# A first weights' page loaded in two halves, the rows' squares behind their splits, and a priority for the values' products of a gated attention

## The chip, the cores and the metric

The kernel runs on one core of one Trainium2 chip. The metric is device time in microseconds (us). Engines are named as the profile names them: PE is TensorE (PEld its weight load), DVE is VectorE, ACT is ScalarE, POOL is GpSimd, SP is SyncE, which here only issues DMAs.

## The reference, cut to what matters

Two transformer blocks follow each other on one sequence of 512 rows and 1024 columns, all in float32. Block 1 puts 16 meta tokens in front and mixes a state-space model with a differential attention; block 2 is a gated linear attention with a mixture of experts, then a sparse attention with another. The change touches the beginning of block 1 and the beginning of block 2:

```python
# block 1
hn = rmsnorm(h, norm1_g)                    # h * rsqrt(mean(h*h) + eps) * g
u, q, k, v, g_ssm, g_att = split(hn @ w_in) # 528 rows, K = 1024
y_ssm = s5_mixer(u, ...)                    # x = B u; complex scan over the rows; y = C s + d u; gelu; GLU
o = diff_attention(q, k, v, lam, slopes)
h = h + (sigmoid(g_ssm) * (y_ssm @ w_ssm_out) + sigmoid(g_att) * (y_att @ w_att_out)) @ w_o
h = h + conv_glu_ffn(rmsnorm(h), ...)
...
# block 2, gated linear attention (gla_mixer)
q, k, v, g_low, r = split(x @ w_in)
log_a = log_sigmoid(g_low @ w_gate_up + b_gate) / 16
b = cumsum(log_a within a chunk of 64 rows)
q_dec = q * exp(b);  k * exp(-b);  k * exp(b_last - b)
o = where(causal, q_dec @ (k * exp(-b)).T, 0) @ v + q_dec @ states
```

## The kernel before, in words

Rows are kept transposed: a tile is 128 of the 1024 features by all rows (528 in block 1, `T`; 512 in block 2, `S`). Every float32 product is made of three products of rounded numbers: each operand is split into a high part (ACT rounds it) and a low part (DVE subtracts), and `mm3` (L394, L395, L396) issues high x high, low x high and high x low, all added up in PSUM.

**Weights** arrive as a stream of pages of 128x2048 (1 MB; tag `wr`, three buffers, `Stream.ahead`, DMA at L334). `Tiles.next` takes 1024 columns at a time and splits them at L369: a CAST on ACT, then a TENSOR_TENSOR on DVE, called the lo split below. There are two such split pairs in flight, and the split is put 1000 places ahead of the program's order. The order of instructions on each engine is fixed when the kernel is built: a scheduler takes the program in the order written, where `tc.high_priority(offset=n)` moves what stands in it n places forward, and models when buffers come free. On the chip an engine keeps to that order and waits where something is not ready.

**Block 1's start.** SP issues the eight loads of `hT` (L454, tiles `hx`), three pages of weights, and the small tables. For each of the eight k, ACT makes the high part `xh` (L461), DVE the low part `xl` (L462), ACT the square (L464), and PE adds up the squares of all k against a tile of ones (L466, `ss`). `rstd_wide` turns that sum into 1/rms (L473 on ACT, L474 RECIPROCAL on DVE). The rows aren't scaled before the product with the weights: the result is multiplied by 1/rms when it is taken out of PSUM (L360). The first four output tiles (`mm`, 48 matmuls of 264 columns each) are `u`; the query and gate tiles follow as filler between the steps of the state-space model.

**The state-space model** works in four groups (`ssm_main`, m = 0 to 3) and three steps each: transposes; then `xps` (L673), a copy by ACT (L675), eight products and two scans by DVE (L680 and around it), six more products, and four DMAs that turn the state round (L688); then `yps` (L700, L701), a copy by ACT (L702), `yt` (L708) and gelu (L709). Fillers stand between the steps. After the last filler come the key and value products (`kv`, 512 columns), whose PSUM tiles are `kv_2269`, `kv_2270` and so on in the orders below.

**Block 2's start.** The rows are split again; eight small products give `glo`, and four more (`z`, L1100) the gate's argument. DVE adds the bias (L1101), ACT makes Abs, Exp and Ln over 128x2048 (L1102, L1103, L1104), DVE four products and four scans (L1108, L1109), ACT three exponentials (L1111, L1112, L1118). The values' products, `stream_tm`, take two halves of 512 columns: each is 96 matmuls of 512 columns into four PSUM banks (`tm`), which are then copied to `vtok` at L1145, two banks by ACT and two by DVE. The second half needs the banks of the first from its 14th matmul on. After them come the eight tiles of queries and keys (`mm`); the first query tile is taken out of PSUM by DVE at L1150.

Of the kernel before, what the change touches and what calls it, by code (L numbers as in the profile page):

```python
# [14 lines left out]
AF = mybir.ActivationFunctionType  # L15
ALU = mybir.AluOpType
# [5 lines left out]
KD = 8  # L22
# [246 lines left out]
def build(ctx, tc, I, out, dbg=None):  # L269
    nc = tc.nc  # L270
    V, A, G, TE = nc.vector, nc.scalar, nc.gpsimd, nc.tensor
# [13 lines left out]
    def sb(n, tag, dt=F32, bufs=1):  # L285
        return ar.get(n, tag, dt, bufs)

    def p2(name):
        return pp_.tile([P, 2, 512], F32, tag="p2", name=name, bufs=3)
# [10 lines left out]
    def load_c(name, dt=F32, eng=None):  # L300
        ap = I[name]
        t = gc.tile([ap.shape[0], ap.shape[1]], dt, tag=name, name=name)
        (eng or nc.sync).dma_start(out=t, in_=ap)
        return t

    def load_a(name, dt=F32):

        ap = I[name]
        t = sb(ap.shape[1], name, dt)[:ap.shape[0]]
        nc.sync.dma_start(out=t, in_=ap)  # L310
        return t
# [6 lines left out]
    class Stream:  # L318
# [9 lines left out]
        def ahead(self, n):  # L328

            for i in range(self.used, min(self.used + n, len(self.src))):  # L330
                if i not in self.tiles:
                    ap, bufs = self.src[i]
                    t = sb(2048, "wr", F32, bufs)
                    ld = nc.sync.dma_start(out=t[:, :ap.shape[1]], in_=ap)  # L334
                    self.later(ld)
                    if i in self.hold:
                        tc.add_manual_dep(ld.ins, self.hold[i], mybir.DependencyInfo(mybir.DependencyClass.Sync, mybir.DependencyReason.DATA),
                                          reason="the rows that are needed sooner go first")
                    self.tiles[i] = t

        def later(self, ld):

            if self.behind is not None:
                after(ld, self.behind)
# [6 lines left out]
    st = Stream()  # L351
# [7 lines left out]
    def tt(o, a, b, op, eng=None):  # L359
        return (eng or V).tensor_tensor(o, a, b, op=op)  # L360
# [32 lines left out]
    def mm3(o, a, b, start, stop):  # L393
        TE.matmul(o, a[0], b[0], start=start, stop=False)  # L394
        TE.matmul(o, a[0], b[1], start=False, stop=False)  # L395
        TE.matmul(o, a[1], b[0], start=False, stop=stop)  # L396
# [24 lines left out]
    def pairs(h, l):  # L421
        def x(k, sl):
            return h[k][:, sl], l[k][:, sl]
        return x
# [26 lines left out]
    hx = [sb(T, "hx", bufs=8) for _ in range(KD)]  # L451
    with tc.manual_schedule(engines={mybir.EngineType.SP}):
        for k in range(KD):
            nc.sync.dma_start(out=hx[k], in_=I['hT'][:, k])  # L454
        st.ahead(WR)
        s_a, s_d = load_c('s_a'), load_c('s_d')
        s_b, s_c = load_a('s_b'), load_a('s_c')
        blk, b16 = load_c('c_blk'), load_c('c_b16')
        g2, glu_b, qks, cw, cb = (load_c(n) for n in ('g2', 'glu_b', 'qks', 'cw', 'cb'))
    for k in range(KD):  # L460
        A.activation(xh[k], hx[k], AF.Identity, scale=g1[:, k:k + 1])  # L461
        V.scalar_tensor_tensor(xl[k], hx[k], g1[:, k:k + 1], xh[k].bitcast(F32), op0=ALU.mult, op1=ALU.subtract)  # L462
        t = sb(T, "t1", bufs=3)
        A.activation(t, hx[k], AF.Square)  # L464
        for j, sl in enumerate(HC):
            TE.matmul(pss[:, j, :264], ones, t[:, sl], start=k == 0, stop=k == KD - 1)  # L466
    drop("hx")
# [109 lines left out]
    for g_ in range(2):  # L577
        for ri in range(2):
            nc.scalar.dma_start(out=bst[64 * ri:64 * ri + 64, g_ * 256:(g_ + 1) * 256],
                                in_=bb[64 * g_:64 * g_ + 64, ri * 256:(ri + 1) * 256])  # L580
# [190 lines left out]
    def proj_kv():  # L771
        acc = [p1("kv0"), p2("kv1"), p2("kv2")]
        o = [acc[0], acc[1][:, 0], acc[1][:, 1], acc[2][:, 0], acc[2][:, 1]]
        for k in range(KD):
            w = wt.next(512)
            for c, (k0, n) in enumerate(kch):
                mm3(o[c], x1(k, slice(k0, k0 + P)), w, k == 0, k == KD - 1)
        return o

    o = proj_kv()  # L780
# [24 lines left out]
    o = proj_kv()  # L805
# [128 lines left out]
    for j in range(16):  # L934
        i, h = j // 4, j % 4
# [62 lines left out]
    for m in range(8):  # L998
        o = sb(T, "h1", bufs=3)[:, :MID]
# [9 lines left out]
        else:  # L1009
            t = sb(T, "t1", bufs=3)[:, :MID]  # L1010
# [9 lines left out]
    hx = pairs(hh, hl)  # L1020
# [3 lines left out]
    for m in range(NFF):  # L1024
# [4 lines left out]
        c = sb(S, "t1", bufs=3)  # L1029
# [11 lines left out]
    for m in range(8):  # L1041
        t = sb(S, "t1", bufs=3)
# [45 lines left out]
    for k in range(KD):  # L1088
        split(x2[k], x2h[k], x2l[k])
        c = k % 4  # L1090
# [31 lines left out]
    def stream_tm(x, mid=None):  # L1122

        acc = [p2("tm0"), p2("tm1")]
        o = [acc[0][:, 0], acc[0][:, 1], acc[1][:, 0], acc[1][:, 1]]
        for k in range(KD):
            w = wt.next(512)
            for t in range(4):
                mm3(o[t], x(k, slice(t * P, (t + 1) * P)), w, k == 0, k == KD - 1)
            if mid and k == 3:  # L1130
                mid()
        return o
# [6 lines left out]
    drop_tiles("xf")  # L1139
    drop("rst", "cu", "gt1", "glo", "w_gl", "w_gu")  # L1140
    vtok = [sb(1024, f"vtok{t}") for t in range(4)]
    for nh in range(2):
        o = stream_tm(xx)
        for t in range(4):
            (A.copy if t % 2 else V.tensor_copy)(vtok[t][:, nh * 512:(nh + 1) * 512], o[t])  # L1145
    for m in range(8):
        ps = dense_fm(KD, xx, [slice(0, S)], p1u)[:, 0]
        sl = slice((m % 4) * S, (m % 4 + 1) * S)
# [561 lines left out]
    o = stream_tm(x4a)  # L1710
# [11 lines left out]
    o = stream_tm(x4a)  # L1722
# [210 lines left out]
    for nh in range(2):  # L1933
        o = stream_tm(x4a, first_half if nh else None)
# [66 lines left out]
```

## Time and profile before

| | |
|---|---|
| median of 3 runs | 1920.88 us (1920.16 to 1924.55) |
| profiled execution, its own time | 1918.51 us |
| its span | 1916.7 us |
| mean granted clock of TensorE, share of full speed | 0.949 |
| PE busy | 1743.3 us, 91% of the span |
| DVE, ACT, POOL busy | 64%, 46%, 9% |

The span is what the profile sees between the first and the last instruction; the time of the same execution is 1.8 us longer. PE is busy for nine tenths of the span, so a step is worth what it takes from PE's idle time or from the stretches in which its clock is at half.

### The profile page before, as it was taken

What the parts mean: (1) busy time and instruction counts of PE and PEld (TensorE: products, weight loads), DVE (VectorE), ACT (ScalarE), POOL (GpSimd) and SP (SyncE); (2) the same over time, 40 slices, a digit from 0 to 9 for tenths busy, and PEclk for the clock granted to TensorE, in tenths of its full rate; (3) what the DMA queues carried; (4) which work ended last, traced back from release to release, by engine and by line L of the source; (5) the groups of instructions that cost most, each with busy time, mean ns of one, the idle gap of its engine ahead of it and who ended that gap; (6) DMA issues with size and microseconds to landing.
All of it is one profiled execution on the core that took longest, in us unless ns stands there. A gap on an engine that the chain in (4) does not pass through costs nothing.

```text
span 1916.7 us, 27254 instructions
## 1 busy us (share of the span) xinstructions
PE 1743.3 (91%) x10719; PEld 1480.1 (77%) x10719; DVE 1221.8 (64%) x2276; ACT 874.1 (46%) x1397; POOL 173.3 (9%) x140
## 2 busy tenths in 40 slices
PE   8999999899999999999999799949998999859990
PEld 7899877798989988877888578738886777647870
DVE  7855368776555643253347889874337777669985
ACT  4233346433333332243223288843236665628881
POOL 2310000022000000000000122110000000012213
PEclk9999999899999999999999799979898999879995
DMA  5335221242322233212225599752230003539953
GB/s 194 110 110 140 89 88 65 63 160 90 108 89 89 88 135 114 95 66 88 88 88 206 188 325 380 281 217 77 85 136 23 1 12 123 208 126 338 380 224 140
DMA packets 69205, 269.73 MB, mean 141 GB/s; under 512 B 22144, under 2 KB 24720, under 8 KB 44240
## 3 DMA queue, kind: packets, MB, share of 16 engines
q1 hardware_dynamic: 52384, 246.38, 35.9%
q0 software_dynamic: 9216, 16.80, 2.4%
q10 hardware_dynamic: 7472, 4.76, 1.2%
q8 instruction: 85, 1.39, 0.3%
q14 instruction: 48, 0.39, 0.1%
HBM read 249.62 MB, written 30.43 MB: 146 GB/s over the span
## 4 chain that ended last, share of the span: by engine, by line
PE 63%; DVE 6%; ACT 3%; DMA 2%; issue 2%; POOL 0%; SPq 0%; POOLq 0%; DVEq 0%; ACTq 0%
PE mm L396 8%; PE mm L395 8%; PE mm L394 8%; PE psh L395 3%; PE psh L396 3%; PE psh L394 3%; PE tm L394 2%; PE tm L395 2%; PE tm L396 2%; PE npo L1920 2%; PE npt L1908 2%; PE op L395 2%; PE op L394 2%; PE op L396 2%; PE xgt L1431 1%
## 5 line engine op out<-in xcount | busy, mean ns | idle before, releaser
L369 ACT CAST pg<-pg 128x1024 fp32r<-128x1024 f32 (+2 forms) x437 | 427.4, 1007 | 554.1 <-PE mm L395 224.9
L369 DVE TENSOR_TENSOR pg<-pg,pg 128x1024 fp32r<-128x1024 f32 (+2 forms) x437 | 503.0, 1176 | 264.6 <-ACT pg L369 251.4
L396 PE MATMUL mm<-pg,pg 128*128 128x258 f32 (+2 forms) x1504 | 483.0, 322 | 4.0 <-DVE pg L369 4.0
L394 PE MATMUL mm<-pg,pg 128*128 128x258 f32 (+2 forms) x1504 | 484.9, 323 | 1.4 <-ACT pg L888 0.7
L395 PE MATMUL mm<-pg,pg 128*128 128x258 f32 (+2 forms) x1504 | 482.9, 321 | 0.0
L394 PEld LDWEIGHTS mm<-pg,pg 128*128 128x128 f32 x1504 | 287.6, 191 | 28.0 <-ACT pg L886 2.8
L396 PEld LDWEIGHTS mm<-pg,pg 128*128 128x128 f32 x1504 | 286.8, 191 | 24.9 <-DVE pg L369 4.7
L395 PEld LDWEIGHTS mm<-pg,pg 128*128 128x128 f32 x1504 | 287.4, 191 | 21.2 <-issue 0.4
L360 DVE TENSOR_TENSOR pg<-mm,pg 128x256 f32<-128x256 f32 (+3 forms) x138 | 66.2, 510 | 138.8 <-PE mm L396 138.8
L395 PE MATMUL psh<-pg,pg 128*128 128x512 f32 x256 | 106.4, 416 | 2.3 <-DVE pg L369 2.3
L394 PE MATMUL psh<-pg,pg 128*128 128x512 f32 x256 | 101.9, 398 | 0.0
L396 PE MATMUL psh<-pg,pg 128*128 128x512 f32 x256 | 101.3, 396 | 0.0
L394 PE MATMUL tm<-pg,pg 128*128 128x512 f32 x192 | 76.4, 408 | 4.6 <-ACT pg L1145 4.6
L395 PE MATMUL tm<-pg,pg 128*128 128x512 f32 x192 | 77.3, 403 | 1.2 <-DVE pg L369 1.2
L396 PE MATMUL tm<-pg,pg 128*128 128x512 f32 x192 | 76.1, 396 | 0.0
L360 DVE TENSOR_TENSOR pg<-pg,pg 128x512 f32<-128x512 f32 (+12 forms) x103 | 57.1, 575 | 24.9 <-ACT pg L675 10.6
L1892 ACT ACTIVATE pg<-ns,nmx 128x512 f32<-128x512 f32 (+3 forms) x128 | 66.3, 531 | 11.4 <-DVE nmx L1888 7.2
L1888 DVE TENSOR_REDUCE nmx<-ns 128x2 f32<-128x1024 f32 (+3 forms) x48 | 50.1, 1043 | 17.3 <-PE ns L1885 17.1
L360 DVE TENSOR_TENSOR pg<-pg 128x64 f32<-128x64 f32 (+8 forms) x127 | 49.5, 411 | 17.4 <-ACT pg L1033 15.4
L395 PEld LDWEIGHTS psh<-pg,pg 128*128 128x128 f32 x256 | 48.9, 191 | 13.2 <-DVE pg L369 4.4
L1425 POOL DMA_INDIRECT pg<-xd,idx x32 | 38.1, 1189 | 219.2 <-DVE wts L360 122.7
L394 PEld LDWEIGHTS psh<-pg,pg 128*128 128x128 f32 x256 | 48.8, 191 | 11.4
(440 smaller groups left out, 2960.9 us busy)
## 6 DMA issues: line engine op xcount, KB each, us to landing
pg<-in_w_moe_dram SPq DMA_DIRECT2D x96, 1024.0 KB, 10.4
pg<-in_w_up_dram SPq DMA_DIRECT2D x22, 1024.0 KB, 4.8
pg<-in_w_dn_dram SPq DMA_DIRECT2D x11, 1024.0 KB, 4.9
pg<-in_w_g_dram SPq DMA_DIRECT2D x8, 1024.0 KB, 5.5
pg<-in_w_go_dram SPq DMA_DIRECT2D x8, 1024.0 KB, 4.8
pg<-yd SPq DMA_DIRECT2D x16, 512.0 KB, 7.8
pg<-in_w_n_dram SPq DMA_DIRECT2D x8, 1024.0 KB, 6.8
pg<-in_w_no_dram SPq DMA_DIRECT2D x8, 1024.0 KB, 4.8
```

What stands on the lines that cost most here:

```text
L360: return (eng or V).tensor_tensor(o, a, b, op=op)
L369: return A.copy(h, src), V.tensor_tensor(l, src, h.bitcast(F32), op=ALU.subtract)
L394: TE.matmul(o, a[0], b[0], start=start, stop=False)
L395: TE.matmul(o, a[0], b[1], start=False, stop=False)
L396: TE.matmul(o, a[1], b[0], start=False, stop=stop)
L1425: ld = G.indirect_dma_start(out=xg, out_offset=None, in_=self.xd, in_offset=bass.IndirectOffsetOnAxis(ap=self.idx[:, e:e + 1], axis=0), bo ...
L1431: TE.transpose(ps[:, k // 4, (k % 4) * P:(k % 4 + 1) * P], xg[:, k * P:(k + 1) * P], ident)
L1888: V.tensor_reduce(mx, sc, axis=AX.X, op=ALU.max, negate=True)
L1892: A.activation(pp[:, r, br], sc[:, r, br], AF.Exp, bias=mx[:, r, br:br + 1], accum_out=se[:, r, br:br + 1])
L1908: TE.transpose(src[:, r, br, c * P:(c + 1) * P], pp[:, r, br, c * P:(c + 1) * P], ident)
L1920: TE.matmul(o_[64 * r:64 * r + 64], vsw[:, c * 512 + br * 256 + g * 64:c * 512 + br * 256 + (g + 1) * 64], pts[r][:, br, c * P:(c + 1) * P ...
```

## The change

Three edits. The first page of `w_u` is loaded in two halves: the first 1024 columns right behind the first two loads of `hT`, the other 1024 behind the eighth. The loop over the eight tiles writes all splits first and all squares in a second loop, and the squares of even k go to DVE as a product. The two halves of the values' products and the copies of their results get a priority of 1000 places.

```diff
+                    c = ap.shape[1] // 2 if i == 0 else ap.shape[1]
+                    ld = nc.sync.dma_start(out=t[:, :c], in_=ap[:, :c])
                     self.later(ld)
+                    if i == 0:
+                        self.first = t, ap, c
...
+        def rest(self):
+            t, ap, c = self.first
+            nc.sync.dma_start(out=t[:, c:2 * c], in_=ap[:, c:])
...
         for k in range(KD):
             nc.sync.dma_start(out=hx[k], in_=I['hT'][:, k])
+            if k == 1:
+                st.ahead(1)
+        st.rest()
         st.ahead(WR)
...
     for k in range(KD):
         A.activation(xh[k], hx[k], AF.Identity, scale=g1[:, k:k + 1])
         V.scalar_tensor_tensor(xl[k], hx[k], g1[:, k:k + 1], xh[k].bitcast(F32), op0=ALU.mult, op1=ALU.subtract)
+    for k in range(KD):
         t = sb(T, "t1", bufs=3)
-        A.activation(t, hx[k], AF.Square)
+        if k % 2:
+            A.activation(t, hx[k], AF.Square)
+        else:
+            tt(t, hx[k], hx[k], ALU.mult)
...
-    for nh in range(2):
-        o = stream_tm(xx)
-        for t in range(4):
-            (A.copy if t % 2 else V.tensor_copy)(vtok[t][:, nh * 512:(nh + 1) * 512], o[t])
+    with tc.high_priority(offset=1000):
+        for nh in range(2):
+            o = stream_tm(xx)
+            for t in range(4):
+                (A.copy if t % 2 else V.tensor_copy)(vtok[t][:, nh * 512:(nh + 1) * 512], o[t])
```

In the changed kernel lines are moved: mm3 is L402, L403, L404, the splits L377, products L368, `ss` L481, `xps` L688, `yps` L715 and L716, `yt` L723, the gate's Abs, Exp and Ln L1117 to L1119, the copies of the values L1161. Because an order built by a scheduler depends on all that stands ahead of it, the first two edits also move instructions far behind the place that they touch. SP's order moves too: the second page of `w_q` now stands four places ahead of where it was among the small tables, and so well ahead of `c_tok`, where before it stood right ahead of it.

At the start, PE before: all sums of squares, then the first product.

```order
L466 MATMUL ss<-pg_102,c_ones 128x264 x4
L466 MATMUL ss<-pg_132,c_ones 128x264 x2
L466 MATMUL ss<-pg_102,c_ones 128x264 x4
L466 MATMUL ss<-pg_132,c_ones 128x264 x2
L466 MATMUL ss<-pg_102,c_ones 128x264 x4
L394 MATMUL mm<-pg_75,pg_430 128x264
L395 MATMUL mm<-pg_77,pg_430 128x264
```

And PE now; `pg_75` and `pg_77` are high and low parts of the rows, `pg_431` holds the split weights.

```order
L481 MATMUL ss<-pg_103,c_ones 128x264 x4
L402 MATMUL mm<-pg_75,pg_431 128x264
L403 MATMUL mm<-pg_77,pg_431 128x264
L481 MATMUL ss<-pg_143,c_ones 128x264 x2
L404 MATMUL mm<-pg_75,pg_431 128x264
L402 MATMUL mm<-pg_75,pg_431 128x264
L403 MATMUL mm<-pg_77,pg_431 128x264
```

The sums of squares, which stood ahead of the first output tile, are now strewn among its matmuls.

At the last group of the state-space model (m = 3), PE before: `xps`, then 14 matmuls `mm` and 48 `kv`, then `yps`. First and last rows of that stretch:

```order
L673 MATMUL xps<-pg_81,pg_380 64x66 x16
L395 MATMUL mm<-pg_78,pg_483 128x256
L396 MATMUL mm<-pg_76,pg_483 128x256
L394 MATMUL mm<-pg_76,pg_483 128x258
L395 MATMUL mm<-pg_78,pg_483 128x258
```

```order
L394 MATMUL kv_2270<-pg_483,pg_75 128x512
L395 MATMUL kv_2270<-pg_483,pg_75 128x512
L396 MATMUL kv_2270<-pg_483,pg_77 128x512
L700 MATMUL yps<-pg_380,pg_81 66x128
L701 MATMUL yps<-pg_403,pg_81 66x128
```

And PE now, where the two steps of the same group almost touch:

```order
L404 MATMUL kv_2271<-pg_484,pg_75 128x512
L402 MATMUL kv_2271<-pg_484,pg_75 128x512
L688 MATMUL xps<-pg_81,pg_381 64x66 x16
L403 MATMUL kv_2271<-pg_484,pg_75 128x512
L404 MATMUL kv_2271<-pg_484,pg_77 128x512
L715 MATMUL yps<-pg_381,pg_81 66x128
L716 MATMUL yps<-pg_404,pg_81 66x128
L715 MATMUL yps<-pg_381,pg_81 66x128
```

The number of matmuls ahead of `yps` is the same as before; 60 of the 62 that stood between the two steps now stand ahead of `xps`.

At the gate of block 2, ACT before: `pg_7091` is the gate's argument, `pg_7107` its running sum, `tm` the values' products.

```order
L1102 ACTIVATE pg_7091<-pg_7090 128x2048
L369 CAST pg_483<-pg_96 128x1024
L1103 ACT_TABLE_LOAD
L1103 ACTIVATE pg_7091<-pg_7091 128x2048
L1104 ACT_TABLE_LOAD
L1104 ACTIVATE pg_7091<-pg_7091 128x2048
L369 CAST pg_430<-pg_92 128x1024
L369 CAST pg_483<-pg_92 128x1024
L1111 ACT_TABLE_LOAD
L1111 ACTIVATE pg_7116<-pg_7107 128x2048
L1112 ACTIVATE pg_7117<-pg_7107 128x2048
L1145 COPY pg_7167<-tm_7169 128x512
```

And ACT now:

```order
L377 CAST pg_431<-pg_86 128x1024
L377 CAST pg_484<-pg_86 128x1024
L1161 COPY pg_7169<-tm_7171 128x512
L1161 COPY pg_7168<-tm_7170 128x512
L1117 ACTIVATE pg_7092<-pg_7091 128x2048
L1118 ACT_TABLE_LOAD
L1118 ACTIVATE pg_7092<-pg_7092 128x2048
L377 CAST pg_431<-pg_95 128x1024
L1119 ACT_TABLE_LOAD
L1119 ACTIVATE pg_7092<-pg_7092 128x2048
```

The copies of the first half's results, which stood behind five passes over the gate, now stand ahead of the first. On PE the second and third `z` have moved behind 48 matmuls of the first half and the fourth behind the first matmul of the second half.

## Rows read from the trace of the kernel before

**Rows 1.** The page: engines' busy time, share of the span and instructions.

```profile
PE 1743.3 (91%) x10719; PEld 1480.1 (77%) x10719; DVE 1221.8 (64%) x2276; ACT 874.1 (46%) x1397; POOL 173.3 (9%) x140
```

**Rows 2.** Timeline, PE at the start: start, length, engine, line, operation [idle before <- releaser].

```profile
6.22 9.99 PE L466 MATMUL ss<-pg,c_ones 128*128 128x264 f32 x32 [6.22 <-ACT pg L464]
15.85 0.48 PE L394 MATMUL mm<-pg,pg 128*128 128x264 f32 x1
```

**Rows 3.** Timeline, ACT at the start.

```profile
14.19 1.98 ACT L369 CAST pg<-pg 128x1024 fp32r<-128x1024 f32 x2
```

**Rows 4.** Timeline, SP's DMA issues at the start.

```profile
0.76 4.26 SPq L454 DMA_DIRECT2D pg<-in_hT_dram  x8
5.06 2.23 SPq L334 DMA_DIRECT2D pg<-in_w_u_dram  x2
...
24.65 0.42 SPq L334 DMA_DIRECT2D pg<-in_w_q_dram  x1
25.12 0.43 SPq L303 DMA_DIRECT2D c_tok<-in_c_tok_dram  x1
```

**Rows 5.** Timeline, DVE at the start.

```profile
15.25 2.36 DVE L369 TENSOR_TENSOR pg<-pg,pg 128x1024 fp32r<-128x1024 f32 x2 [1.76 <-ACT pg L369]
18.36 3.45 DVE L474 RECIPROCAL pg<-pg 128x528 f32<-128x528 f32 x1 [0.75 <-ACT pg L473]
...
30.00 0.17 DVE L1059 TENSOR_SCALAR tok<-c_tok 128x4 f32<-128x4 f32 x1 [3.51 <-DMA c_tok<-in_c_tok_dram]
```

**Rows 6.** Waits between 30 and 90 us: total us, times, longest.

```profile
PE mm L396 <- DVE pg L369: 4.0, 3, 2.2
```

**Rows 7.** Windows: length, busy us of PE, PEld, DVE, ACT, POOL, granted clock, DMA.

```profile
28.00:52.00 24.00, 19.92 (x161) 19.30 (x160) 21.97 (x77) 4.21 (x8) 13.01 (x9) 1.00 0.31 93
...
84.00:204.00 120.00, 119.08 (x1097) 116.25 (x1096) 62.92 (x138) 39.20 (x58) 17.17 (x19) 0.99 0.43 128
```

**Rows 8.** Timeline, the last group of the state-space model, all engines.

```profile
203.59 0.92 PE L673 MATMUL xps<-pg,pg 128*64 128x66 f32 x25
...
206.22 0.40 PE L394 MATMUL kv<-pg,pg 128*128 128x512 f32 x1
...
206.60 0.75 DVE L360 TENSOR_TENSOR pg<-mm,pg 128x258 f32<-128x258 f32 x2
...
208.22 1.19 DVE L369 TENSOR_TENSOR pg<-pg,pg 128x1024 fp32r<-128x1024 f32 x1
...
212.36 0.65 ACT L833 ACTIVATE pg<-pg 128x528 f32<-128x528 f32 x1 [5.01 <-DVE pg L360]
...
217.34 0.38 PE L700 MATMUL yps<-pg,pg 128*66 128x128 f32 x2
```

**Rows 9.** The four DMAs of that group (L688): issue, and time to landing.

```profile
L688 ACTq DMA_DIRECT2D pg<-pg x4: 468/526/632, 211.2 to 213.0; - x4
...
DMA to landing us min/median/max: 3.1/3.8/4.4
```

**Rows 10.** Timeline, PE in the values' products.

```profile
858.32 0.50 PE L395 MATMUL tm<-pg,pg 128*128 128x512 f32 x1 [1.16 <-DVE pg L369]
...
865.90 0.80 PE L394 MATMUL tm<-pg,pg 128*128 128x512 f32 x1 [4.57 <-ACT pg L1145]
```

**Rows 11.** Window behind that wait, columns as in rows 7.

```profile
865.00:871.00 6.00, 5.10 (x12) 4.05 (x13) 1.46 (x3) 3.14 (x4) 0.00 (x0) 0.50 0.48 175
```

**Rows 12.** Timeline, ACT at the gate.

```profile
844.15 1.92 ACT L1102 ACTIVATE pg<-pg 128x2048 f32<-128x2048 f32 x1 [2.65 <-DVE pg L1101]
...
865.28 1.05 ACT L1145 COPY pg<-tm 128x512 f32<-128x512 f32 x2
```

**Rows 13.** Timeline, DVE at the gate and at the first query tile.

```profile
853.52 2.50 DVE L1108 SCALAR_TENSOR_TENSOR pg<-pg,pg 128x512 f32<-128x512 f32 x4 [5.23 <-ACT pg L1104]
...
858.19 3.44 DVE L1109 TENSOR_TENSOR_SCAN pg<-pg,pg 128x512 f32<-128x512 f32 x3
...
893.15 0.69 DVE L1150 SCALAR_TENSOR_TENSOR pg<-mm,pg 128x512 f32<-128x512 f32 x1 [3.19 <-PE mm L396]
```

More of the change, by code (lines that the diff above doesn't have):

```diff
@@ L333, in ahead @@
                     t = sb(2048, "wr", F32, bufs)
-                    ld = nc.sync.dma_start(out=t[:, :ap.shape[1]], in_=ap)
+                    c = ap.shape[1] // 2 if i == 0 else ap.shape[1]
+                    ld = nc.sync.dma_start(out=t[:, :c], in_=ap[:, :c])
                     self.later(ld)
+                    if i == 0:
+                        self.first = t, ap, c
                     if i in self.hold:
```

## The prediction

> **What bounds the kernel now.** I read the page first. PE is busy 91% of the span [rows 1], so the end moves by what the change adds to or takes from PE's waits and half-clock stretches. The edits work in two places, so I read the timelines of each: the start, then, since the order of instructions moves far behind it, PE's order up to 225 us; and the gate of block 2.
>
> At the start PE adds up squares from 6.22 us on, each fed by ACT, and its first product with weights comes at 15.85 us [rows 2], because ACT splits the first page last, from 14.19 us on [rows 3]. Then PE is not the limit: from 28 to 52 us DVE is busy 21.97 of 24 us, PE 19.92 [rows 7], and PE waits 4.0 us in three places for lo splits of weights [rows 6]. In this stretch a product starts when DVE has got to its lo split. DVE itself stands 3.51 us before 30.00 us, behind a small table, `c_tok`, whose load was issued right behind a 1 MB page [rows 4, 5]. From 84 us on PE is full, 119.08 of 120 us [rows 7]: a lead that PE has at 84 us is carried unchanged to 204 us.
>
> At the gate PE waits 1.16 us and then 4.57 us; the second wait ends with ACT's copy of the first half's results, which had to let the exponentials pass [rows 10, 12]. After it 12 matmuls run with a granted clock of 0.50, the lower of TensorE's levels (1.2 GHz) [rows 11].
>
> **The start, part by part.** *Two halves of the page.* The pages were issued from 5.06 us on, behind all of `hT`, whose eight issues take 4.26 us from 0.76 on [rows 4]. The first half is now issued behind two of them, about 1.8 us in. The loads of `hT` landed 2.8 to 5.6 us after their issue; taking 5.6 us and a little for twice the bytes, the half page is there at about 7.6 us, and the later `hT` loads about 1.2 us later than before (estimates). ACT and DVE can split it among the rows. So PE's first product can start about 6 us earlier. But PE had not been idle: the squares took it 9.99 us from 6.22 [rows 2]. They are 32 passes, now strewn among the first tile's 48 matmuls. 9.99 / 32 is 0.31 us with waits on ACT in it, the later ones follow at 0.22 us; 32 of these are 7.1 us. 48 matmuls at 0.12 us (14 `mm` in 204.51 to 206.22 [rows 8]) are 5.8 us. Waiting on ACT for the last rows (about 15.0 us) and on DVE for the second half's lo split (about 16.9 us, since `xl` and four products stand ahead of it), PE ends the second output tile at about 26.5 us; before, 15.85 + 2 x 5.8 = 27.5 us. That is a gain of **1 us**, not 6.
>
> *Squares behind the splits.* No work is removed. Four squares move from ACT to DVE, about 0.7 us each, where DVE had waited for ACT. The sum of squares ends at about 19.5 us instead of 16.2, so RECIPROCAL starts about 2.1 us later than its 18.36 [rows 5]. That is a loss, and PE's evictions wait for it; three PSUM pairs cover it.
>
> *What DVE gets back.* The second page of `w_q` is now issued ahead of four tables, and `c_tok` lands at about 27 us, when DVE, after the late RECIPROCAL, is only about there. The 3.51 us fall away and 2.1 us are lost: 1.4 us. Beside this the lo splits stand about 2 us of small operations further ahead in DVE's order. Together the lo split that PE needs before it fills comes **3.4 us** earlier; that is PE's lead at 84 us. Bounds: 1 us (only the first tile's gain survives), and 7.4 us, which is what the order itself assumes: 61 more dense matmuls stand ahead of each step of the state-space model, at 0.12 us.
>
> *What the order does with it.* This is the costliest term, and the diff doesn't show it. Before, between the last group's `xps` (ends at 204.51) and its `yps` (starts at 217.34 without a wait) PE had 14 `mm` and 48 `kv` matmuls, at 0.23 us each of the latter [rows 8]. In the new order two `kv` are left there, 0.5 us. Between the two steps lies a chain that no engine can shorten: ACT's copies, 12 products and two scans on DVE, four DMAs. It ran from 204.51 to the last landing: issued at 213.0, plus at least 3.1 us [rows 9], 216.1. That is 11.6 us; in it DVE also did two evictions (0.75) and one lo split (1.19) [rows 8], which now stand elsewhere: 9.7 us. Without ACT's 0.65 us between the DMAs [rows 8] it would be 9.0. PE has 0.5 us to do meanwhile, so it stands for 9.7 - 0.5 = **9.2 us** (8.5 to 11.1). The number of matmuls ahead of `yps` is unchanged, so the lead is set against this: 9.2 - 3.4 = 5.8 us later.
>
> Then the clock. After the 4.57 us wait at the gate 12 matmuls took 0.43 us a step instead of 0.23, 2.4 us lost [rows 10, 11]. The new wait is twice as long, and what follows it is as light as `yps`, `yt` and the wait for gelu, so I take **2.5 us** (0 to 4). The Trainium skill ("TensorE: Matmul & The Clock Gate", section "HAM oscillation — how this bites in real kernels") describes just this, a wait for a transfer between bursts of matmuls after which the clock is at the lower level; it speaks against the start of this change, and rows 11 agree with it. Without it the sum below would be 2.5 us less.
>
> **The values' products.** At a higher priority the copies stand ahead of the gate's five passes. That removes the 4.57 us, the 2.4 us of low clock and the earlier wait of 1.16 us: 8.1 us. The price is that the gate is late: Abs started at 844.15 [rows 12], now it needs the fourth `z`, which stands behind the first half. The first half ends at about 856.2 (before about 858.2: less the wait of 1.16 and one `z` of about 0.9), so Abs starts at about 859.3. Abs to the four products took 853.52 - 844.15 = 9.4 us, with one CAST in it as now; then the products 2.50 and three scans 3.44 [rows 13], and only behind these, in DVE's order, the second half's last lo split, 1.2 us: 875.8. The second half gets there after 0.9 + 72 x 0.23 = 17.4 us, at 873.6, and can do its products with the high part meanwhile. A new wait of about **1.5 us** (0 to 3.5). Net 8.1 - 1.5 = **6.6 us** gained (4 to 8.1), read where the first query tile leaves PSUM: 893.15 [rows 13] becomes 886.5. What comes next is PE work without a wait, so the gain is kept.
>
> **Sum.** +9.2 (stall) - 3.4 (lead) + 2.5 (clock) - 6.6 (gate) = +1.7 us on the profiled execution's 1918.51 us, 1920.2. That execution stands 2.4 us under the median of the runs, 1920.88, so the time is about 1922.5 us. Differences under 0.3% (5.8 us) are what a measurement of this kernel can't tell from no change.
>
> **The rivals.** *A: the start gives all that the order assumes.* With a lead of 7.4 us the sum is 9.2 - 7.4 + 2.5 - 6.6 = -2.3: 1918.6 us. Against it: DVE's busy share up to 84 us [rows 7]; the squares still need PE. Still "same".
> *B: the stall isn't there.* If the state's DMAs land before PE arrives, for instance since PE is late and the chain's DVE work is not queued behind anything, only lead and gate count: -3.4 - 6.6 = -10, about 1911 us. Against it: `yps` reads what the DMAs bring, `xps` begins the chain, and two matmuls are all that stands between.
> *C: slower.* The lead is spent at once: if RECIPROCAL's delay reaches PE through the evictions, or `c_tok` still lands late, the lead is 1 us or less; the stall is 10 to 11 us and the clock stays low through `yps` and `yt` (3.5). With a gate gain of 5.5, 10.5 - 0.5 + 3.5 - 5.5 = +8: about 1929 us. It decides as soon as the lead is under 1.5 us while the gate gives less than 6. For it: PE waits for DVE in this stretch already [rows 6].
> *D: the change doesn't do what it says.* The half page lands early but ACT, with no time free between the rows, splits it no earlier than now. That is lead 0 and else the forecast: +5.1, 1926 us.
>
> **How the numbers follow.** Forecast and A, 0.62 together (0.47 and 0.15): within 0.3%. B, or a lead and a gate gain both at their best with no loss of clock: 0.18, faster. C 0.14, and the worse half of D 0.06: slower, 0.20. The range from 1912 to 1930 us leaves out the far ends of B and C, some 0.15.
>
> **What would show it.** In the profile after: the first product at about 9 to 11 us, the last sum of squares about 19.5; DVE's wait for `c_tok` gone; PE ahead by 3 to 4 us at 84 us; a wait of `yps` for a DMA of 8.5 to 11 us near 214 to 223 us, behind it a stretch at half clock; no wait of `tm` for ACT's copies, one of 1 to 2 us for a lo split near 874 us; the first query tile taken out about 6.6 us earlier in relation to block 2's start. The prediction is wrong if `yps` doesn't wait, if the lead is over 7 us or negative, or if PE's order at run time finds other buffers late.

## The result, and the profile after

The change makes the kernel slower. The median of the changed kernel is 1937.82 us (5 runs, 1935.58 to 1941.27) against 1924.12 us (5 runs) before; the ratio is 1.0077, 95% interval 1.0058 to 1.0097. A second set on another occasion gave 1933.48 us (12 runs) against 1921.40: 1.0052 [1.0030, 1.0074]. So the change costs 14 and 12 us by the medians, where the forecast was 1.7 us, too little to tell from no difference.

The two profiled executions are 21.5 us apart in span, 1938.2 against 1916.7. That is more than the medians: the profiled execution of before, 1918.51 us, was under all five of its runs, and that of the changed kernel, 1939.97 us, the second longest of its five. PE is busy 11.6 us longer with the same 10719 matmuls, and idle for the rest of the 21.5 us; the totals don't say where (page of the changed kernel, first part; before in [rows 1]):

```profile
PE 1754.9 (91%) x10719; PEld 1490.0 (77%) x10719; DVE 1221.7 (63%) x2280; ACT 872.3 (45%) x1393; POOL 175.3 (9%) x140
```

To see where the time went, the table sets both traces beside each other by work: all matmuls up to a point, each weighed with its usual step in the trace of before, give an amount of work, and the table says how many us later (+) or earlier (-) another kernel had done that amount. Where the order differs just there, as at 214.5 us, a value depends on the weights by up to 1 us. The kernels beside the changed one are those of the experiments.

| before at, us | changed | again | start only | priority only | halves only | squares only | cover 48 | cover 48 plus 4 |
|---|---|---|---|---|---|---|---|---|
| 74 | -4.3 | -5.2 | -2.7 | -0.6 | -2.8 | -2.5 | -5.3 | -5.5 |
| 115 | +1.9 | -0.2 | +2.0 | -0.4 | -1.7 | -3.8 | -1.1 | -1.9 |
| 214.5 | 0.0 | -2.1 | +0.1 | -1.3 | -1.3 | -3.2 | -0.4 | -1.3 |
| 232 | +11.2 | +9.2 | +11.4 | -1.3 | -0.3 | -2.2 | +0.7 | -0.3 |
| 346 | +12.6 | +10.5 | +12.8 | +0.1 | -0.3 | +7.5 | +2.3 | -0.3 |
| 808 | +11.7 | +9.7 | +12.0 | -0.8 | -2.4 | +5.4 | +1.1 | -2.4 |
| 882 | +3.2 | +1.2 | +11.9 | -9.4 | -2.5 | +5.4 | -7.5 | -11.0 |
| 892 | +7.3 | +5.3 | +11.9 | -5.3 | -2.5 | +5.4 | -3.4 | -6.9 |
| 1001 | +7.3 | +5.3 | +11.9 | -5.3 | -2.5 | +5.4 | -3.4 | -6.9 |
| 1011 | +15.5 | +13.5 | +11.9 | +2.9 | -2.5 | +5.4 | +4.8 | -6.9 |
| 1100 | +15.9 | +14.4 | +11.1 | +3.7 | -3.2 | +6.3 | +5.6 | -8.3 |
| 1112 | +20.9 | +19.3 | +13.7 | +7.9 | +3.2 | +11.4 | +9.6 | -1.2 |
| 1862 | +21.8 | +16.5 | +15.4 | +9.1 | +4.7 | +12.2 | +11.4 | -0.1 |

Four steps carry the changed kernel's column. **Between 214 and 232 us** it loses 11.2 us in the table. The timeline of the last group of the state-space model (start, length, engine, line, operation [idle before <- releaser]; it answers to [rows 8]):

```profile
216.74 1.15 PE L688 MATMUL xps<-pg,pg 128*64 128x66 f32 x32
...
217.47 0.85 ACT L690 COPY pg<-xps 128x264 f32<-128x264 f32 x2 [3.71 <-PE xps L688]
...
222.91 1.12 ACTq L703 DMA_DIRECT2D pg<-pg  x2
...
224.47 1.12 ACTq L703 DMA_DIRECT2D pg<-pg  x2
...
226.54 0.66 PE L715 MATMUL yps<-pg,pg 128*66 128x128 f32 x2 [7.99 <-DMA pg<-pg]
...
232.81 0.72 PE L723 MATMUL yt<-c_ident,pg 66*128 66x66 f32 x8 [0.67 <-ACT pg L717]
```

`yps`, which found its data ready before, now waits 7.99 us for the DMAs, and from there to `yt` it takes 6.27 us instead of 4.32 (217.34 to 221.66). The windows (columns as in [rows 7]) show why: the granted clock fell during the wait, and `yps` begins at the lower level. Ahead of this `yps` stand 1685 matmuls in both kernels. They are done at 217.34 us before and at 226.54 - 7.99 = 218.55 us now, so PE was 1.2 us behind when the wait began; 8.0 us of wait and 2.0 us of slower `yps` make up the rest of the 11.2 us.

```profile
218.50:226.50 8.00, 0.05 (x1) 0.00 (x0) 5.84 (x15) 1.53 (x2) 0.00 (x0) 0.82 0.20 48
226.50:230.50 4.00, 3.96 (x19) 3.99 (x20) 0.31 (x2) 0.60 (x2) 0.00 (x0) 0.50 0.02 5
```

**Between 808 and 892 us** it gains 4.4 us. Both waits of [rows 10] are gone, and one new wait has come, on a lo split that stands behind three scans on DVE; ACT had ended the CAST of that split 5 us earlier. Timelines of ACT, DVE and PE there, and the window behind the wait:

```profile
880.74 1.03 ACT L377 CAST pg<-pg 128x1024 fp32r<-128x1024 f32 x1
```

```profile
883.28 3.45 DVE L1124 TENSOR_TENSOR_SCAN pg<-pg,pg 128x512 f32<-128x512 f32 x3
886.65 1.20 DVE L377 TENSOR_TENSOR pg<-pg,pg 128x1024 fp32r<-128x1024 f32 x1
```

```profile
887.90 0.50 PE L403 MATMUL tm<-pg,pg 128*128 128x512 f32 x1 [2.22 <-DVE pg L377]
```

```profile
888.00:893.00 5.00, 5.00 (x15) 3.97 (x16) 4.61 (x7) 3.99 (x3) 0.00 (x0) 0.66 0.62 210
```

**Between 1001 and 1011 us** it loses 8.2 us without a wait. Here PE does the small products of the gated attention (`go`, `grs`) with which its output begins. The changed kernel's windows, then those of before, from about the same point of the work on:

```profile
1007.00:1014.00 7.00, 7.00 (x43) 7.00 (x42) 2.49 (x12) 0.85 (x1) 0.95 (x1) 0.62 0.09 33
1014.00:1021.00 7.00, 7.00 (x35) 7.00 (x34) 1.41 (x2) 0.17 (x1) 0.00 (x0) 0.50 0.14 44
```

```profile
1000.00:1007.00 7.00, 7.00 (x65) 7.00 (x64) 3.89 (x14) 1.02 (x1) 0.95 (x1) 1.00 0.24 77
1007.00:1014.00 7.00, 6.55 (x51) 5.85 (x50) 5.21 (x15) 1.97 (x2) 0.00 (x0) 1.00 0.00 1
```

In the changed kernel PE is busy all the time, 7.00 of 7.00 us in both windows, and yet gets through 43 and 35 matmul records instead of 65 and 51 (in before the second window has room left, 6.55 of 7.00 us), because the granted clock is at the lower level.

**Between 1100 and 1112 us** it loses 5.0 us in the first gathers of the mixture of experts. Waits of PE there, before and then after:

```profile
PE xgt L1431 <- DMA pg<-xd,idx: 6.5, 2, 6.3
```

```profile
PE xgt L1447 <- DMA pg<-xd,idx: 10.5, 2, 6.2
```

Over all fourteen profiles these waits add up to 6.5 us in that of before, 6.8 in `after_cover24` and 8.5 to 11.4 in the twelve others, `halves_only` among them (11.4), which loses nothing else up to there. So the profile of before was most likely lucky with its gathers, and I don't count these 5 us as an effect of the change; without them the profiles are 16.5 us apart, nearer to what the medians say.

### The profile page after: what moved, and what is told of

Its sections match the earlier page's. It is cut to its first block, busy times and chain, and to the rows that moved or that the text cites. A ratio compares the mean times of both kernels' runs of the same rounds, so it can differ in the third digit from the quotient of the medians.

```text
span 1938.2 us, 27247 instructions
## 1 busy us (share of the span) xinstructions
PE 1754.9 (91%) x10719; PEld 1490.0 (77%) x10719; DVE 1221.7 (63%) x2280; ACT 872.3 (45%) x1393; POOL 175.3 (9%) x140
## 4 chain that ended last, share of the span: by engine, by line
PE 63%; DVE 7%; ACT 2%; DMA 2%; issue 2%; POOL 0%; POOLq 0%; SPq 0%; DVEq 0%; ACTq 0%
PE mm L404 8%; PE mm L403 8%; PE mm L402 8%; PE psh L403 3%; PE psh L404 3%; PE psh L402 3%; PE tm L403 2%; PE tm L402 2%; PE tm L404 2%; PE npo L1936 2%; PE npt L1924 2%; PE op L403 2%; PE op L402 2%; PE op L404 2%; PE xgt L1447 1%
## 5 line engine op out<-in xcount | busy, mean ns | idle before, releaser
L377 ACT CAST pg<-pg 128x1024 fp32r<-128x1024 f32 (+2 forms) x437 | 427.6, 1007 | 571.8 <-PE mm L403 233.3
L377 DVE TENSOR_TENSOR pg<-pg,pg 128x1024 fp32r<-128x1024 f32 (+2 forms) x437 | 503.2, 1176 | 270.4 <-ACT pg L377 257.2
L402 PE MATMUL mm<-pg,pg 128*128 128x258 f32 (+2 forms) x1504 | 485.8, 323 | 1.5 <-ACT pg L903 0.7
L404 PE MATMUL mm<-pg,pg 128*128 128x258 f32 (+2 forms) x1504 | 484.0, 323 | 2.8 <-DVE pg L377 2.8
L403 PE MATMUL mm<-pg,pg 128*128 128x258 f32 (+2 forms) x1504 | 484.3, 322 | 0.0
L402 PEld LDWEIGHTS mm<-pg,pg 128*128 128x128 f32 x1504 | 288.6, 192 | 28.6 <-ACT pg L901 2.7
L404 PEld LDWEIGHTS mm<-pg,pg 128*128 128x128 f32 x1504 | 288.0, 191 | 24.2 <-DVE pg L377 3.6
L403 PEld LDWEIGHTS mm<-pg,pg 128*128 128x128 f32 x1504 | 288.4, 192 | 21.5 <-issue 0.6
L368 DVE TENSOR_TENSOR pg<-mm,pg 128x256 f32<-128x256 f32 (+3 forms) x138 | 66.4, 511 | 138.6 <-PE mm L404 138.6
L403 PE MATMUL psh<-pg,pg 128*128 128x512 f32 x256 | 106.7, 417 | 2.3 <-DVE pg L377 2.3
L402 PE MATMUL psh<-pg,pg 128*128 128x512 f32 x256 | 102.0, 398 | 0.0
L404 PE MATMUL psh<-pg,pg 128*128 128x512 f32 x256 | 101.5, 396 | 0.0
L403 PE MATMUL tm<-pg,pg 128*128 128x512 f32 x192 | 77.1, 401 | 2.2 <-DVE pg L377 2.2
L368 DVE TENSOR_TENSOR pg<-pg,pg 128x512 f32<-128x512 f32 (+12 forms) x103 | 56.2, 571 | 33.8 <-ACT pg L632 13.3
L404 PE MATMUL tm<-pg,pg 128*128 128x512 f32 x192 | 76.0, 396 | 0.0
L402 PE MATMUL tm<-pg,pg 128*128 128x512 f32 x192 | 75.4, 403 | 0.0
L368 DVE TENSOR_TENSOR pg<-pg 128x64 f32<-128x64 f32 (+9 forms) x131 | 51.8, 418 | 20.8 <-ACT pg L1048 15.4
L1904 DVE TENSOR_REDUCE nmx<-ns 128x2 f32<-128x1024 f32 (+3 forms) x48 | 50.1, 1044 | 20.9 <-PE ns L1901 20.8
L403 PEld LDWEIGHTS psh<-pg,pg 128*128 128x128 f32 x256 | 48.9, 191 | 13.3 <-DVE pg L377 4.4
L1447 PE MATMUL xgt<-c_ident,pg 128*128 128x128 f32 x256 | 38.7, 301 | 21.3 <-DMA pg<-xd,idx 21.2
```

What stands on the lines that cost most here:

```text
L377: return A.copy(h, src), V.tensor_tensor(l, src, h.bitcast(F32), op=ALU.subtract)
L1447: TE.transpose(ps[:, k // 4, (k % 4) * P:(k % 4 + 1) * P], xg[:, k * P:(k + 1) * P], ident)
L1904: V.tensor_reduce(mx, sc, axis=AX.X, op=ALU.max, negate=True)
```

## The experiments

Ratios are to runs of the kernel before in the same set; brackets are 95% intervals.

| kernel | median us | before us | ratio |
|---|---|---|---|
| start_only | 1931.85 | 1924.22 | 1.0040 [1.0027, 1.0052] |
| prio_only | 1924.92 | 1924.22 | 0.9994 [0.9978, 1.0011] |
| halves_only | 1924.10 | 1924.22 | 1.0004 [0.9994, 1.0014] |
| squares_only | 1930.33 | 1924.22 | 1.0035 [1.0023, 1.0048] |
| after_again | 1933.48 | 1921.40 | 1.0052 [1.0030, 1.0074] |
| after_cover24 (one run) | 1921.97 | 1921.40 | - |
| after_cover48 | 1926.76 | 1921.40 | 1.0015 [0.9993, 1.0037] |
| halves_prio | 1920.26 | 1921.40 | 0.9995 [0.9976, 1.0014] |
| prio_plus4 | 1915.24 | 1922.39 | 0.9960 [0.9940, 0.9981] |
| before_plus4 | 1926.89 | 1922.39 | 1.0026 [1.0008, 1.0044] |
| halves_prio_plus12 | 1921.15 | 1922.39 | 0.9986 [0.9959, 1.0013] |
| cover48_plus4 | 1920.64 | 1919.40 | 1.0005 [0.9986, 1.0025] |

### The edits one by one

`start_only` is the changed kernel with this taken back:

```diff
-    with tc.high_priority(offset=1000):
-        for nh in range(2):
+    for nh in range(2):
```

> The kernel before with both edits of the start (page in halves, squares in their own loop) and without the priority of the values' products. Theory 1 (the order): PE has two kv matmuls between the last group's xps and yps here too, so yps waits about 8 us for the state's DMAs and the clock falls behind it; at 240 us the kernel is 10 to 12 us later than before, and the time is 9 to 13 us longer (ratio 1.005 to 1.007). Theory 2 (the later half-clock stretches near 1010 and 1100 us in the changed kernel belong to the start's shift): the same wait, and besides the half-clock stretches near 1010 and 1110 us, together 18 us or more. Theory 3 (they belong to the priority at the gate): the wait, and a profile that behind 900 us looks like that of the kernel before.

The wait is there with the same length, and the table's column stays at +11 to +13 from 232 us to 1100 us; nothing is lost near 1010 us. The time is 7.6 us longer, a little less than theory 1 said. The first line of `yps`:

```profile
226.56 0.66 PE L715 MATMUL yps<-pg,pg 128*66 128x128 f32 x2 [7.97 <-DMA pg<-pg]
```

Theory 2 falls: the start's edits alone don't bring the half clock near 1010 us. The loss at the last group is theirs.

`prio_only` is the kernel before with the priority alone.

> The kernel before with the priority of the values' products alone. Theory 1: the wait of 4.6 us for ACT's copies is gone, a wait of about 2 us for a lo split behind the scans and a half-clock stretch of 3.4 us behind it take its place; the first query tile comes about 4.4 us earlier in relation to block 2's start, and the time is 3 to 5 us shorter (ratio 0.9975 to 0.9985). Theory 3 (the priority brings the later half-clock stretches): the same gain at 900 us, then 8 us lost near 1010 us and about 5 near 1100, and a time 5 to 9 us longer.

Gain and loss both come as theory 3 said: -5.3 us at 892 us, and +8.2 between 1001 and 1011 us. Neither theory's time came: the ratio, 0.9994, lies between the two, and the runs lie wide apart, 1910 to 1928 us.

`halves_only` and `squares_only` split the start's edits:

```diff
     for k in range(KD):
         A.activation(xh[k], ...)
         V.scalar_tensor_tensor(xl[k], ...)
+    for k in range(KD):            # squares_only; not in halves_only
         t = sb(T, "t1", bufs=3)
```

> The kernel before with the page in two halves alone; squares stay on ACT and in their place. The order built from it has 15 mm and 48 kv matmuls between the last xps and yps, as before. Theory 1: yps doesn't wait, no half clock near 224 us, and the time is within 3 us of before: ACT is busy from 4.9 us on and takes the early half page up only among the rows. Theory 2' (the start itself costs the time, whatever the cover): 3 us or more longer.

> The kernel before with the squares in their own loop, even k on DVE, and nothing else. The order has 14 mm and 48 kv matmuls between the last xps and yps, as before. Theory 1: yps doesn't wait; the first products wait for ACT's split of the page behind the splits of the rows, a little earlier than before; the time is within 3 us of before. Theory 2' (the start itself costs): 3 us or more longer, since the squares' sum and with it the reciprocal come later.

Both keep the cover, and `yps` waits in neither: it takes both edits together to lose it. `halves_only` is within 0.15% of before. `squares_only` is a miss: it is 6.1 us slower, where theory 1 allowed 3. That is what theory 2' said, but not where it said it: the kernel is 3.2 us ahead at 214 us and then loses 9.7 us between 300 and 346 us, in the attention, far from the edit. There 96 matmuls `mm` stand 8 to 20 places further back in PE's order than before, behind parts of the softmax ahead of which they had stood. PE comes to these parts sooner and has less to do while it waits; 13.7 us of this stretch run at the lower clock. That the order is the cause was read from the traces and not tested. Windows of `squares_only`, then of before, from about the same work on:

```profile
296.00:306.00 10.00, 8.53 (x48) 6.63 (x47) 9.72 (x36) 5.78 (x17) 0.00 (x0) 0.84 0.23 74
306.00:330.00 24.00, 21.17 (x109) 16.99 (x108) 16.52 (x52) 10.49 (x31) 0.00 (x0) 0.78 0.11 36
```

```profile
298.00:308.00 10.00, 9.38 (x61) 7.26 (x60) 9.31 (x36) 5.60 (x16) 0.00 (x0) 1.00 0.31 106
308.00:332.00 24.00, 22.08 (x147) 17.17 (x146) 22.19 (x67) 16.16 (x45) 0.00 (x0) 1.00 0.15 45
```

### The lost cover, put back in two doses

An order-only tie holds the first matmul of each kv accumulator (or of the last two) behind the last `xps`, so that PE's order has 48 (or 24) `kv` between `xps` and `yps` instead of 2.

```diff
-                mm3(o[c], x1(k, slice(k0, k0 + P)), w, k == 0, k == KD - 1)
+                i = mm3(o[c], x1(k, slice(k0, k0 + P)), w, k == 0, k == KD - 1)
+                if xlast[0] is not None and k == 0 and c in (0, 1, 2, 3, 4):   # (3, 4) in after_cover24
+                    after(i, xlast[0].ins.name)
```

> The changed kernel, with one order-only tie: the first matmul of each kv accumulator is placed behind the last group's xps. PE's order then has 48 kv matmuls between the last xps and yps, as before the change (the order of the first tiles differs little). Theory 1 (the lost cover is what the start's edits cost): yps doesn't wait, no half clock near 224 us; at 240 us the kernel is at most 3 us behind the kernel before instead of 11, and the time is 7 to 11 us shorter than the changed kernel's. Rival (the chain of the last group is late for another reason, so that a cover only moves the wait to yt or xps): PE waits as long at another place, and at 240 us it is still 8 us or more behind.

> The changed kernel, with the tie on two of the five kv accumulators alone: 24 kv matmuls between the last xps and yps instead of 2, 5.1 us more. Theory 1: the wait of yps falls by as much, from 8.0 to about 2.9 us (2 to 4). Rival: the wait stays at 7 us or more, because the chain starts later by what was put in between.

> The changed kernel unchanged, a second profile of it and times on the same chip as the others of this set. By the first profile: yps waits 8 us, tm waits 2.2 us for a lo split. If the half-clock stretch that began at 1009 us and the wait of 4.3 us for a gather at 1121 us belong to the change, they are there again with the same length; if they come and go with the run, at least one of them is missing or differs by 3 us or more, and runs of the time differ by as much.

The first line of the last `yps` with 24 and with 48 matmuls, and in the repeated profile of the changed kernel:

```profile
220.45 0.66 PE L718 MATMUL yps<-pg,pg 128*66 128x128 f32 x2 [3.31 <-DMA pg<-pg]
```

```profile
216.89 0.38 PE L718 MATMUL yps<-pg,pg 128*66 128x128 f32 x2
```

```profile
224.55 0.67 PE L715 MATMUL yps<-pg,pg 128*66 128x128 f32 x2 [8.10 <-DMA pg<-pg]
```

So the wait is 8.10 us in the repeated profile; with 24 matmuls (5.1 us more) it is 3.31 and with 48 nothing. The dose fits to within 0.4 us: the wait is the chain's length less what PE has to do. At 232 us the kernel with 48 is 0.7 us behind before instead of 9.2 to 11.2, and its median is 6.7 us under that of the changed kernel in the same set (1926.76 against 1933.48; 7 to 11 were expected). The profiles show this part of the loss; the times agree, but the runs of both kernels spread over 19 us and more.

The repeated profile also has the 8.2 us near 1010 us again, and the long wait for the gathers (11.2 us), so these aren't a chance of one run.

### The half clock near 1000 us

`halves_prio`, the two edits that seemed free or useful, was to be the better version.

> The page in two halves and the priority of the values' products, squares as before. Theory 1: the gains of the two single edits add up, 2.4 us at 260 us and 4 to 5 at 900 us, about 7 us, and the half-clock stretch near 1000 us comes or not by the run: 1912 to 1920 us where it doesn't, 8 us more where it does; ratio 0.996 to 1.000. Theory 3 (the priority brings this stretch in every run): no run under 1920.

It was 8.2 us ahead at 1001 us and lost 6.5 of them in the same place; the median is no better than before, though six of its twelve runs are under 1920 us. Theory 3 had said that none would be; but the profiled execution, one of the six with 1919.66 us, has the stretch at half clock (window below), so that bound couldn't tell the theories apart.

```profile
991.00:1008.00 17.00, 17.00 (x94) 15.97 (x93) 5.22 (x20) 1.02 (x1) 0.95 (x1) 0.62 0.10 33
```

By now the stretch had been at half clock in all six profiles with the priority and in none of the four without. Yet in before and `prio_only` PE's instructions of the 16 us ahead of the first `grs` are the same, and their times relative to it agree within 0.03 us; so do those of DVE, ACT and POOL. What differs is when the stretch comes. Theory 4 was made from that, and tested both ways: four more matmuls, 0.9 us, in the kernel with the priority and in the kernel before.

```diff
+            for _ in range(more if k == 0 else 0):   # more = 4 (or 12) for the first query tile of block 2
+                TE.matmul(ps[:, 0, :512], w[0], x(k, cols[0])[0], start=True, stop=True)
```

> The priority alone, and the first product of the first query tile of block 2 done four times more before it counts (each starts its sum anew, so the result is the same): 0.9 us of dense work between the gate and the stretch of small matmuls (go, grs) near 1000 us. In all six profiles with the priority TensorE's clock fell there, in none of the four without it, though PE's order ahead of it is the same. Theory 4 (it is the moment at which the stretch comes, which the priority moves by the waits that it takes away): 0.9 us more bring it to about the moment that it has without the priority, the stretch runs at full clock, and the time is about 6 us shorter than with the priority alone, 1915 to 1921 us. Theory 3' (something that the priority changes in the order or the buffers): the stretch is at half clock for 14 to 17 us again and the time 1 us longer.

> The kernel before with the same four matmuls more, 0.9 us. Theory 4: the stretch of small matmuls near 1000 us now comes at a moment at which the clock falls (as it did in the changed kernel with 24 kv matmuls, where it came 0.6 us later than in the kernel before in relation to the clock's earlier falls): 14 to 17 us at half clock there, and a time 5 to 9 us longer than before. Theory 3': no half clock there, 1 us longer.

> The page in halves and the priority, with twelve such matmuls more, 2.8 us, which by theory 4 carry the stretch past the moment at which the clock fell in halves_prio. Theory 4: full clock near 1000 us, and in spite of 2.8 us more work 3 to 6 us less time than halves_prio. Theory 3': half clock as there, 3 us longer.

The window over the stretch in four kernels: `prio_only`, `prio_plus4`, before, `before_plus4`.

```profile
994.00:1011.00 17.00, 17.00 (x88) 16.56 (x88) 4.54 (x18) 1.02 (x1) 0.95 (x1) 0.57 0.10 33
```

```profile
996.00:1013.00 17.00, 16.54 (x137) 15.66 (x136) 10.07 (x30) 2.99 (x3) 0.95 (x1) 1.00 0.10 33
```

```profile
1000.00:1017.00 17.00, 16.55 (x137) 15.68 (x136) 10.05 (x30) 3.00 (x3) 0.95 (x1) 1.00 0.10 32
```

```profile
1000.00:1017.00 17.00, 17.00 (x90) 15.97 (x90) 7.51 (x27) 2.03 (x2) 0.95 (x1) 0.60 0.09 32
```

The same 0.9 us of needless work takes the half clock away in one kernel and brings it into the other. `prio_plus4` is faster than before, 0.9960 [0.9940, 0.9981], although the same edit without the four matmuls is not; `before_plus4` is 4.5 us slower than before. What theory 4 said of these two came: the same edit works one way in one kernel and the other way in the other, so it isn't the four matmuls themselves, and the moment at which the stretch comes is what they share. `halves_prio_plus12` is a miss: its stretch ran at half clock too (from 997 us on for 17 us, 1921.15 us), so the theory doesn't say beforehand which moments are bad.

The traces' records of the granted clock support the moment in another way. From the clock's last rise to the first `grs` it is 115.2 and 115.4 us in `prio_plus4` and `cover48_plus4`, and 128.8 to 129.0 us in before, `start_only`, `halves_only` and `squares_only`: all six at full clock. It is 114.4 us in the changed kernel, its repetition, `prio_only` and `after_cover48`, 117.5 in `halves_prio_plus12`, 129.8 in `before_plus4` and 539.2 in `halves_prio` and `after_cover24`: all eight at half clock. Bad distances lie below, between and above the good ones, twice within 1 us of them, so it isn't simply how long the clock had been up that decides. What the chip looks at isn't settled by these runs.

`cover48_plus4` takes both causes out of the changed kernel.

> The changed kernel with both causes taken away that the runs so far name: the tie that puts 48 kv matmuls back between the last xps and yps, and the four matmuls more behind the values' products (0.9 us), which shift the stretch of small matmuls against the clock's falls as in prio_plus4. Theory 1 with theory 4 (these two are the whole loss): no wait of yps, full clock near 1000 us, at 1010 us of the kernel before 2 to 4 us ahead of it, and a time 5 to 8 us under after_cover48, 1916 to 1922 us, ratio 0.996 to 1.000. Rival (a third cost is hidden in the start's edits): full clock there, but a time that is still over 1925 us and a ratio over 1.002.

```profile
993.00:1010.00 17.00, 16.55 (x136) 15.69 (x136) 10.20 (x31) 3.00 (x3) 0.95 (x1) 1.00 0.11 37
```

There is no wait of `yps`, the granted clock is 1.00 from 993 to 1010 us, the kernel is 6.9 us ahead of before at 1011 us (2 to 4 expected), and the median is 6.1 us under that of `after_cover48`; that is another set, and in relation to before it is 4.1 us. The ratio, 1.0005 [0.9986, 1.0025], lies just above the 0.996 to 1.000 that theory 1 with theory 4 expected. So with both causes taken away the kernel is no longer slower than before, but of the 6.9 us that the profile is ahead at 1011 us the times show nothing. The profile loses 7.1 us between 1100 and 1112 us, where PE waits 11.3 us for the gathers; whether that is what other runs lose is open. `prio_plus4` is the only version that beats both kernels.

## Why the prediction was wrong, point by point

- **First product, first tile.** Right: 8.92 us (forecast 9 to 11), the last squares until 20 us (19.5), and at 29 us of before a lead of 0.9 us (1.0), although the first product came 6.9 us earlier (15.85 us in [rows 2]).

```profile
4.99 3.85 PE L481 MATMUL ss<-pg,c_ones 128*128 128x264 f32 x8 [4.99 <-DMA c_ones<-in_c_ones_dram]
8.92 0.39 PE L402 MATMUL mm<-pg,pg 128*128 128x264 f32 x1
```

- **What DVE gets back.** Wrong, 1.4 us of the lead. `c_tok` still makes DVE wait, 2.81 us instead of the 3.51 of [rows 5], since its load was issued at 26.38 us, later than before; and RECIPROCAL is 2.75 us late (forecast 2.1).

```profile
21.11 3.45 DVE L489 RECIPROCAL pg<-pg 128x528 f32<-128x528 f32 x1 [0.75 <-ACT pg L488]
...
30.50 0.17 DVE L1074 TENSOR_SCALAR tok<-c_tok 128x4 f32<-128x4 f32 x1 [2.81 <-DMA c_tok<-in_c_tok_dram]
```

- **The lead of 3.4 us, carried to 204 us.** The lead was 4.3 us at 74 us, but that it came near the forecast there is partly luck, since the term of `c_tok` in it was wrong. At 84 us, the place that the forecast names, the same reckoning gives 1.5 us, 3.8 in the repeated profile and 0.8 in `start_only`. By 115 us it was used up in the changed kernel: two waits on DVE, each with a stretch at half clock behind it (73.5 to 76.9 and 107.6 to 114.4 us; before has one from 103.0 to 106.4). When the work ahead of the last `yps` was done, the changed kernel was 1.2 us behind and the repeated profile 0.9 us ahead. The failed sentence is that a lead "is carried unchanged to 204 us", which I read from PE's busy share of before; the change gave PE waits there that before had not.

```profile
73.42 0.57 PE L404 MATMUL mm<-pg,pg 128*128 128x258 f32 x1 [1.96 <-DVE pg L377]
```

```profile
106.57 1.66 PE L744 MATMUL qss<-c_blk,pg 128*16 128x2 f32 x13 [1.50 <-DVE pg L679]
```

- **The stall and the clock behind it.** The mechanism was right, the size a little under: 7.99 and 8.10 us (9.2; bounds 8.5 to 11.1), and 2.0 us of low clock in `yps` (2.5), 10.0 us in all where the forecast had 11.7. The chain has six products on either side of the scans in the traces, twelve as the forecast counted, not eight and six. The chain's DMAs landed 1.9 us behind their issue (before in [rows 9]), where the forecast took 3.1.

```profile
DMA to landing us min/median/max: 1.9/1.9/1.9
```

- **The values' products.** The mechanism was right to the instruction: the copies' wait gone, the new wait of 2.22 us (1.5) on the lo split behind the three scans. The half clock behind the new wait was left out, though the same paragraph counts it behind the old one: 4.4 us gained instead of 6.6.
- **"What comes next is PE work without a wait, so the gain is kept."** This is the step that failed most. There was no wait, as said, but 8.2 us were lost behind it near 1010 us, because the granted clock fell to 0.50 for 17 us with PE busy; `prio_only` has the same 8.2 us with the priority alone. The loss was no part of the sum and of no rival. Without it the other errors would have left the profile at about +7 us.

Put together from the forecast's +1.7 us: 4.6 for the lead (1.2 us behind instead of 3.4 ahead), -1.7 for stall and clock, 2.2 at the gate and 8.2 near 1010 us make +15.0; the profile has +15.9 at 1100 us. Rival C named the right side and the lead as a cause, and put the size at +8; about half of the loss lay outside all rivals.

The rule that was quoted, that a wait between bursts of matmuls puts the clock back (the Trainium skill, "TensorE: Matmul & The Clock Gate", section "HAM oscillation — how this bites in real kernels"), agrees with the tail of the state-space model, where PE waited 7.99 us for transfers and the granted clock behind it was 0.50. Behind the new wait at the gate the clock fell too, though that wait was 2.22 us and the waits of the section's example are 3 to 5 us. Near 1010 us there was no wait in the records, PE busy 7.00 of 7.00 us, and the clock fell all the same.

## What to carry to other kernels

Where a scheduler fixes the order, an edit is to be read in the order it leads to far behind it: both start edits were cheap where they stand, and cost 11 us (together) and 10 us (the squares alone) in places 200 to 300 us later, where work had been moved that covered a chain (tested for the two together, read from the order for the squares). Count, for each long chain off PE, how much PE work stands between its two ends, before and after. And don't book a gain of a few microseconds as kept while light stretches of PE work lie ahead: moving such a stretch by 0.9 us turned 6 to 8 us on or off, so a measurement of such an edit needs a second version with the moment shifted before the edit is judged by it.

## What the runs showed of the hardware that was not expected

- The granted clock fell to the lower level (1.2 GHz) in a stretch in which PE was busy without a gap in the trace (7.00 of 7.00 us), with 128x1, 128x64 and 128x128 products, and stayed there for 14 to 17 us; the same instructions in the same rhythm ran at full clock when the stretch came 0.9 us later (`prio_plus4`) or earlier (before against `before_plus4`). The fall came 1.6 us behind the start of the first `grs` in the changed kernel, its repetition, `after_cover48` and `prio_only` alike, and 3.3 to 3.6 us in `after_cover24`, `halves_prio` and `before_plus4`, so it is repeatable and not a chance of the run (2.0 us in `halves_prio_plus12`).
- Runs of one kernel in one set differ by 4 us (`start_only`, 1929.71 to 1933.88) to 27 us (`halves_prio_plus12`, 1904.86 to 1932.33); those of before by 7 us in one set (1920.69 to 1928.03) and by 18 in another (1909.77 to 1927.91).
- The same gathers made PE wait 6.5 us in one profile and up to 11.4 in others (before against `halves_only`); why is open.
